# PEER's dense columns on one core: two output chunks per PSUM tile, a column-major first block, and a list and early products moved

## The chip, the cores and the metric

The kernel runs on one core of a Trainium2 chip. The metric is the device time of one execution in microseconds. The kernel before has three timed runs, with a median of 3780.73 us (3780.49 to 3784.08). All durations below come from one further execution that the hardware profiler recorded.

## What is computed

One residual block over 512 tokens of width 2048, then a final RMSNorm. The first half mixes tokens with two kinds of attention; the change doesn't touch it. The second half is PEER, which picks 16 of 16384 single-neuron experts for each token and head:

```python
def peer_ffn(h, w_query, sub_keys, expert_u, expert_v):
    ...
    scores = jnp.einsum('thpc,hpnc->thpn', q, sub_keys.astype(jnp.float32))
    s1, i1 = lax.top_k(scores[:, :, 0], PEER_TOPK)
    s2, i2 = lax.top_k(scores[:, :, 1], PEER_TOPK)
    ...
    top_score, pos = lax.top_k(cand_score, PEER_TOPK)
    expert_ids = jnp.take_along_axis(cand_id, pos, axis=-1)
    gates = jax.nn.softmax(top_score, axis=-1)
    ...
        u_sel = expert_u[idb]
        act = jax.nn.gelu(jnp.einsum('thkd,td->thk', u_sel, xb).astype(jnp.float32))
        w = (gb * act).astype(xb.dtype)
        v_sel = expert_v[idb]
        return jnp.einsum('thk,thkd->td', w, v_sel)
```

The output is `rms_norm(x + peer_ffn(rms_norm(x)))`.

## The kernel before

Activations are kept transposed: 16 chunks of 128 features on the partitions, tokens along the free axis. Every matrix product is done in three matmuls on split numbers (mm3, lines 116 to 118): hi weight by hi activation, hi by lo, lo by hi. A weight block of 128x2048 comes in two halves of 128x1024 (wload, from line 97). For each half a DMA issued by SyncE fills wr, ScalarE rounds it to wh (line 108), and VectorE subtracts to get wl (line 109). There are three buffers each for wh and wl, so a new half waits until PE has finished with an old one.

PEER is done in two ways. For the last 160 tokens the chosen expert rows are gathered by indirect DMAs, and VectorE multiplies each row of 128x2048 (lines 565 to 594). The function pace releases one such row at a time behind wl's and behind adds, so the rows fill VectorE while PE works. For the first 352 tokens (TD) everything is dense. The 16384 experts are 128 columns of 128:

- An up-product of column c is `expert_up(c)`: 48 matmuls of 352 columns into psu, then Gelu into a buffer gl. The first NS = 54 of the 128 are done early, inside the stages that choose the experts and scatter the gates, and their gl are spilled to DRAM (gact_sp). They are read back later by `fetch`. The rest run inside the down stage.
- `weigh(n)` multiplies gl by the gates of column n, which come from a DRAM matrix gsp (through gg, which lies in spare columns of h2), and splits the product into wg hi (ScalarE, line 825) and wg lo (VectorE, line 826). There are four gl buffers, so a spilled column is loaded only when an older one has been weighted.
- The down stage has 16 groups of GC = 8 columns. A group has eight weight blocks (jb), each with two output chunks (jj); the half w[jj] of a block holds chunk jj for all eight columns. A chunk sums 24 matmuls in psy, and VectorE adds it to acc (line 846). psy has four buffers of one PSUM bank.

A scheduler fixes the order of the instructions on each engine beforehand, from the order of the code, the buffers and its own costs. Each engine then takes its instructions strictly in that order.

The stages of PEER, in the profile's time: queries, and choose for the last 160 tokens, until 1578 us; the second loop over the heads, with choose for the 352 tokens and five early ups per head, until 1914; the transposes and the scatter, with one early up in two of three token blocks, until 2114; then the down stage until 3754, the final norm and the store.

Ahead of the second loop stand two pieces that the change moves. The first makes h2 from acc (lines 738 to 743, name h2n). The second builds the gather list of the 32 extra tokens (lines 748 to 763): rep and spread on VectorE, one product psrep on PE, and then idx_b, ggate_b and rstd_b out of it on VectorE.

The inner loop of the down stage, before:

```python
            for jj in range(JJ):
                j = jb * JJ + jj
                ps = (py, py2)[j % 2].tile([P, T], F32, tag="py", name="psy")
                for c in range(GC):
                    ...
                add = nc.vector.tensor_tensor(acc[:, j, :TD], acc[:, j, :TD], ps[:, :TD], op=ALU.add)
                pace(add, 1.0 / JJ)
```

Of the kernel before, what the change touches and what calls it, by code (L numbers as in the profile page):

```python
# [8 lines left out]
F32 = mybir.dt.float32  # L9
# [3 lines left out]
AF = mybir.ActivationFunctionType  # L13
ALU = mybir.AluOpType
# [4 lines left out]
P = 128  # L19
T = 512  # L20
NT = T // P
D = 2048
KC = D // P
# [17 lines left out]
HT = NT - 2  # L41
CW = 112
UPS = 5
NS = NH * UPS + TD // TB - -(-(TD // TB) // 3)
SLOW = 0.8
LEAD = 1
NP = 4
# [3 lines left out]
def block_kernel(ctx, tc, xT, gains, w_vf, bf, w_qk, w_v, w_g, w_br, w_o, w_q, keysT, uT, vP, expert_u, expert_v, outT):  # L51
# [63 lines left out]
    def mm3(ps, wh, wl, ah, al, start, stop):  # L115
        nc.tensor.matmul(ps, wh, ah, start=start, stop=False)  # L116
        nc.tensor.matmul(ps, wh, al, start=False, stop=False)  # L117
        nc.tensor.matmul(ps, wl, ah, start=False, stop=stop)  # L118
# [499 lines left out]
    def early(n, pace=None):  # L618
        for _ in range(n):
            if len(started) < NS:  # L620
                c = len(started)
                nc.scalar.dma_start(gact_sp[c], expert_up(c, pace))
                started.append(c)

    with ExitStack() as s1:
# [88 lines left out]
        for h in range(NH):  # L714
            sc = []
            sv = se.tile([P, 2, HT, NK], F32, tag="sv", name="sv")
            for p in range(2):
                b = 2 * h + p
                if b == 1:
                    norm2()  # L720
                if b == 3:
                    token_rows(lambda k: acc[:, k, T - P:], h2g, accg)
                ps = pu.tile([P, T], F32, tag="pu", name="psq2")
                proj(ps, wload(w_q[b]), h2)
                q = se.tile([P, T], F32, tag="ab1", name="q2")
                nc.scalar.activation(q, ps, AF.Copy)
                kt = se.tile([P, NK], F32, tag="kt", name="kt")
                nc.sync.dma_start(kt, keysT[b])
                ps = psx.tile([P, NT, NK], F32, tag="psx", name="pss")
                for t in range(NT):  # L730
                    nc.tensor.matmul(ps[:, t], q[:, t * P:(t + 1) * P], kt, start=True, stop=True)
                nc.scalar.activation(sv[:, p], ps[:, :HT], AF.Copy)
                sc.append(ps[:, HT:])
            nc.scalar.dma_start(scores[h], sv)
            choose(h, sc, HT, NT - HT)


        for k in range(KC):
            tmp = gl.tile([P, TD], F32, tag="gl", name="h2n")
            nc.vector.scalar_tensor_tensor(tmp, acc[:, k, :TD], g_sb[:, KC + k:KC + k + 1], rstd[:, :TD], op0=ALU.mult,  # L740
                                           op1=ALU.mult)
            nc.scalar.activation(h2[:, k, 0, :TD], tmp, AF.Copy)
            nc.vector.tensor_tensor(h2[:, k, 1, :TD], tmp, h2[:, k, 0, :TD].bitcast(F32), op=ALU.subtract)


        nc.vector.scalar_tensor_tensor(idx, ia[:, NT - 1], float(NK), ib[:, NT - 1], op0=ALU.mult, op1=ALU.add)
        nc.vector.tensor_copy(ggate, gt[:, NT - 1])
        rep = se.tile([P, 2 * HK + 2], F32, tag="ab1", name="rep")
        nc.vector.scalar_tensor_tensor(rep[:, :HK], ia[:, NT - 2], float(NK), ib[:, NT - 2], op0=ALU.mult, op1=ALU.add)
        nc.vector.tensor_copy(rep[:, HK:2 * HK], gt[:, NT - 2])  # L750
        nc.vector.tensor_copy(rep[:, 2 * HK:], rstd_t[:, NT - 2:NT - 1].to_broadcast([P, 2]))
        spread = se.tile([P, GB, MB], F32, tag="kt", name="spread")
        nc.vector.tensor_copy(spread, ident[:, P - MB:].unsqueeze(1).to_broadcast([P, GB, MB]))
        ps = psx.tile([P, T], F32, tag="psx", name="psrep")
        nc.tensor.matmul(ps[:, :2 * HK + 2], spread.rearrange("p g m -> p (g m)"), rep, start=True, stop=True)
        for g in range(GB):
            rows = slice(g * MB, (g + 1) * MB)
            nc.vector.tensor_copy(idx_b[rows], ps[rows, g * SB:(g + 1) * SB])
            nc.vector.tensor_copy(ggate_b[rows], ps[rows, HK + g * SB:HK + (g + 1) * SB])
        nc.vector.tensor_copy(rstd_b, ps[:, 2 * HK:2 * HK + 1])  # L760
        nc.vector.tensor_copy(sel_b, ident[:, :MB])
        for g in range(1, GB):
            nc.vector.tensor_tensor(sel_b, sel_b, ident[:, g * MB:(g + 1) * MB], op=ALU.add)


        for h in range(NH):
            sv = se.tile([P, 2, HT, NK], F32, tag="sv", name="svl")
            nc.sync.dma_start(sv, scores[h])
            choose(h, [sv[:, p] for p in range(2)], 0, HT)
            early(UPS, pace)  # L770

        tr = []
        for n, src in enumerate((ia, ib, gt)):
# [8 lines left out]
        for tb in range(TD // TB):  # L782
            st = se.tile([P, NK, TB], F32, tag="st", name="st")
            for t4 in range(0, TB, 4):
                tk = slice(tb * TB + t4, tb * TB + t4 + 4)
                ab = [se.tile([P, 4, NK], F32, tag=f"ab{i}", bufs=2, name="ab") for i in range(2)]
                nc.vector.tensor_tensor(ab[1], i128.unsqueeze(1).to_broadcast([P, 4, NK]),
                                        tr[1][:, tk].unsqueeze(2).to_broadcast([P, 4, NK]), op=ALU.is_equal)
                ps = pg.tile([P, 4, NK], F32, tag="pg", name="psgt")
                for i in range(4):  # L790
                    t = tb * TB + t4 + i
                    nc.vector.tensor_scalar(ab[0][:, i], i128, tr[0][:, t:t + 1], tr[2][:, t:t + 1], op0=ALU.is_equal,  # L792
                                            op1=ALU.mult)
                    nc.tensor.matmul(ps[:, i], ab[0][:, i], ab[1][:, i], start=True, stop=True)
                nc.scalar.activation(st[:, :, t4:t4 + 4].rearrange("p n t -> p t n"), ps, AF.Copy)
            nc.gpsimd.dma_start(gsp[:, tb], st)
            if tb % 3:
                early(1, pace)

    ex = pool("exp", 1)  # L800
    extra.append(ex)
# [31 lines left out]
    for grp in range(NG):  # L833
        while len(ws) < GC:
            ws.append(weigh(grp * GC + len(ws)))
        for jb in range(KC // JJ):
            w = wload(vP[grp, jb])
            for jj in range(JJ):
                j = jb * JJ + jj
                ps = (py, py2)[j % 2].tile([P, T], F32, tag="py", name="psy")  # L840
                for c in range(GC):
                    b = jj * GC + c
                    wh, wl = w[b // 8]
                    cc = slice(b % 8 * P, (b % 8 + 1) * P)
                    mm3(ps[:, :TD], wh[:, cc], wl[:, cc], ws[c][:, 0], ws[c][:, 1], c == 0, c == GC - 1)
                add = nc.vector.tensor_tensor(acc[:, j, :TD], acc[:, j, :TD], ps[:, :TD], op=ALU.add)
                pace(add, 1.0 / JJ)
        ws = []
    while todo:
        pace(add, 1.0)  # L850
# [81 lines left out]
```

## Time and profile before

| what | value |
|---|---|
| median of three runs | 3780.73 us |
| profiled execution: its own time | 3777.61 us |
| profiled execution: span | 3775.9 us |
| TensorE's mean granted clock | 0.988 of full |
| TensorE busy | 3670.2 us, 97%, 20745 matmuls |
| VectorE busy | 2597.2 us, 69% |
| ScalarE busy | 1290.8 us, 34% |
| DMA, mean over the span | 219 GB/s |

The busy share is taken over the span, which is what the profiler sees between the first and the last instruction. The execution's own time is 1.7 us longer. Matmuls overlap in the array, so the length printed for one is about twice its distance to the next.

### The profile page before, as it was taken

The numbers are of one execution on the slowest core, as the hardware profiler recorded it, in microseconds if no ns is written. First come the engines' busy times: TensorE is split into PE (matmuls) and PEld (weight loads), VectorE is DVE, ScalarE is ACT, GpSimd is POOL, SyncE is SP. The second block draws the span as 40 slices with busy tenths as digits, with TensorE's granted clock in tenths as the row PEclk, the third lists the DMA queues.
The fourth block names the chain that finished last, engine by engine and source line by source line (L and its number), as shares of the span: only waits on it lengthen the run. The fifth ranks groups of instructions, "written<-read, shape, count | busy, mean of one in ns | idle before, by whom it ended". The sixth has DMA issues, their size and how long they took to land.

```text
span 3775.9 us, 52068 instructions
## 1 busy us (share of the span) xinstructions
PE 3670.2 (97%) x20745; PEld 3381.2 (90%) x20745; DVE 2597.2 (69%) x3971; ACT 1290.8 (34%) x1824; POOL 530.6 (14%) x432
## 2 busy tenths in 40 slices
PE   9999999999999999899999898999999999999997
PEld 7888888888887878699999898999999999999997
DVE  5333445444555446899589888888789888988785
ACT  4334222232223223355356432333333333333333
POOL 0000000000000000011001122222223322322320
PEclk9999999999999999999999999999999999999999
DMA  4222222222224232377767899999889889989883
GB/s 142 79 78 77 98 95 95 87 90 81 88 95 138 95 101 97 106 267 275 274 245 274 290 340 326 353 342 331 318 334 372 327 334 337 366 330 343 327 306 110
DMA packets 233700, 827.25 MB, mean 219 GB/s; under 512 B 21736, under 2 KB 82664, under 8 KB 189680
## 3 DMA queue, kind: packets, MB, share of 16 engines
q1 hardware_dynamic: 174032, 450.30, 34.4%
q0 software_dynamic: 49920, 360.74, 24.9%
q10 hardware_dynamic: 9504, 12.88, 0.9%
q8 instruction: 163, 2.67, 0.3%
q14 instruction: 81, 0.66, 0.1%
HBM read 784.72 MB, written 39.11 MB: 218 GB/s over the span
## 4 chain that ended last, share of the span: by engine, by line
PE 83%; DVE 9%; DMA 4%; issue 2%; ACT 1%; SPq 0%; POOL 0%; DVEq 0%; POOLq 0%; ACTq 0%
PE psy L118 7%; PE psy L117 7%; PE psu L118 7%; PE psu L116 7%; PE psu L117 7%; PE psy L116 7%; PE psg L118 3%; PE psg L117 3%; PE psg L116 3%; PE psq L117 3%; PE psq L118 3%; PE psq L116 3%; DVE wl L109 2%; DVE ab L792 2%; PE psk L118 2%
## 5 line engine op out<-in xcount | busy, mean ns | idle before, releaser
L108 ACT ACTIVATE wh<-wr 128x1024 fp32r<-128x1024 f32 x768 | 813.8, 1060 | 1948.6 <-PE psy L117 583.1
L109 DVE TENSOR_TENSOR wl<-wr,wh 128x1024 fp32r<-128x1024 f32 x768 | 936.3, 1221 | 588.7 <-ACT wh L108 586.7
L116 PE MATMUL psy<-wg,wh 128*128 128x352 f32 x2048 | 667.5, 326 | 29.5 <-ACT wg L825 28.7
L117 PE MATMUL psy<-wg,wh 128*128 128x352 f32 x2048 | 670.5, 328 | 8.6 <-DVE wg L826 8.6
L118 PE MATMUL psu<-h,wl 128*128 128x352 f32 x2048 | 665.3, 325 | 12.8 <-DVE wl L109 12.7
L118 PE MATMUL psy<-wg,wl 128*128 128x352 f32 x2048 | 668.8, 328 | 7.4 <-DVE wl L109 7.2
L116 PE MATMUL psu<-h,wh 128*128 128x352 f32 x2048 | 666.5, 325 | 0.0
L117 PE MATMUL psu<-h,wh 128*128 128x352 f32 x2048 | 662.3, 323 | 0.0
L116 PEld LDWEIGHTS psy<-wg,wh 128*128 128x128 f32 x2048 | 389.8, 190 | 31.8 <-ACT wg L825 30.3
L117 PEld LDWEIGHTS psy<-wg,wh 128*128 128x128 f32 x2048 | 390.4, 191 | 10.5 <-DVE wg L826 10.4
L118 PEld LDWEIGHTS psu<-h,wl 128*128 128x128 f32 x2048 | 385.0, 188 | 16.3 <-DVE wl L109 16.3
L118 PEld LDWEIGHTS psy<-wg,wl 128*128 128x128 f32 x2048 | 389.7, 190 | 10.2 <-DVE wl L109 10.0
L117 PEld LDWEIGHTS psu<-h,wh 128*128 128x128 f32 x2048 | 386.2, 189 | 0.0
L116 PEld LDWEIGHTS psu<-h,wh 128*128 128x128 f32 x2048 | 385.9, 188 | 0.0
L558 POOL DMA_INDIRECT row<-eu,idx x128 | 180.8, 1413 | 903.0 <-DVE row L565 585.3
L583 DVE SCALAR_TENSOR_TENSOR acc<-row,gact,acc 128x2048 f32<-128x2048 f32 x128 | 300.2, 2346 | 9.3 <-DMA row<-ev,idx 9.2
L565 DVE SCALAR_TENSOR_TENSOR row<-row,rstd_t,h2g 128x2048 f32<-128x2048 f32 x128 | 300.3, 2346 | 0.0
L558 POOL DMA_INDIRECT row<-ev,idx x128 | 201.6, 1575 | 493.2 <-DVE acc L583 443.6
L116 PE MATMUL psq<-h,wh 128*128 128x512 f32 x512 | 205.2, 401 | 8.4 <-ACT wh L108 8.4
L117 PE MATMUL psq<-h,wh 128*128 128x512 f32 x512 | 206.1, 402 | 0.3 <-DVE h L167 0.3
L118 PE MATMUL psq<-h,wl 128*128 128x512 f32 x512 | 205.3, 401 | 0.1
L118 PE MATMUL psg<-h,wl 128*128 128x512 f32 x512 | 203.8, 398 | 0.0
(313 smaller groups left out, 5481.1 us busy)
## 6 DMA issues: line engine op xcount, KB each, us to landing
wr<-uT SPq DMA_DIRECT2D x256, 512.0 KB, 6.1
wr<-vP SPq DMA_DIRECT2D x256, 512.0 KB, 7.3
wr<-w_qk SPq DMA_DIRECT2D x64, 512.0 KB, 3.5
wr<-w_g SPq DMA_DIRECT2D x64, 512.0 KB, 3.5
gsp<-st POOLq DMA_DIRECT2D x22, 1024.0 KB, 4.5
wr<-w_br SPq DMA_DIRECT2D x32, 512.0 KB, 3.1
wr<-w_o SPq DMA_DIRECT2D x32, 512.0 KB, 3.2
wr<-w_q SPq DMA_DIRECT2D x32, 512.0 KB, 3.7
```

The lines of the kernel that those rows point to most:

```text
L108: nc.scalar.activation(hi, raw, AF.Copy)
L109: ins = nc.vector.tensor_tensor(lo, raw, hi.bitcast(F32), op=ALU.subtract)
L116: nc.tensor.matmul(ps, wh, ah, start=start, stop=False)
L117: nc.tensor.matmul(ps, wh, al, start=False, stop=False)
L118: nc.tensor.matmul(ps, wl, ah, start=False, stop=stop)
L558: nc.gpsimd.indirect_dma_start(out=row.rearrange("p k q -> p (k q)"), out_offset=None, in_=table, in_offset=bass.IndirectOffsetOnAxis(ap=i ...
L565: nc.vector.scalar_tensor_tensor(row, row, rstd_t[:, NT - 1:NT], h2g, op0=ALU.mult, op1=ALU.mult, accum_out=gact[:, i:i + 1])
L583: nc.vector.scalar_tensor_tensor(accg, row, gact[:, i:i + 1], accg, op0=ALU.mult, op1=ALU.add)
L792: nc.vector.tensor_scalar(ab[0][:, i], i128, tr[0][:, t:t + 1], tr[2][:, t:t + 1], op0=ALU.is_equal, op1=ALU.mult)
```

## The change

Five edits, none of which adds or removes a matmul:

1. MORE = 3: 57 up-products are early, not 54; the three more come after the scatter loop, and the first weighting after them.
2. h2n is written inside the first loop over the heads, ahead of the last head's choose.
3. The list of the 32 tokens becomes a function, second_list, which is called in the second loop after the first head's choose and its five early ups.
4. A weight block of the down stage has one psy tile of two neighbouring PSUM banks, one for each chunk. One VectorE instruction of 128x2x352 adds both, and pace is called once per block with 1.0 in place of twice with 0.5. There are two such tiles.
5. In the first block (jb = 0) of each group the matmuls go column by column: for each c, first chunk 0, then chunk 1. The other blocks keep chunk 0 in full before chunk 1.

```diff
+MORE = 3
+NS = NH * UPS + TD // TB - -(-(TD // TB) // 3) + MORE
...
+            if h == NH - 1:
+
+                for k in range(KC):
+                    tmp = gl.tile([P, TD], F32, tag="gl", name="h2n")
...
             choose(h, sc, HT, NT - HT)
...
+        def second_list():
...
             choose(h, [sv[:, p] for p in range(2)], 0, HT)
             early(UPS, pace)
+            if h == 0:
+                second_list()
...
             if tb % 3:
                 early(1, pace)
 
+        early(MORE, pace)
+
...
             w = wload(vP[grp, jb])
-            for jj in range(JJ):
-                j = jb * JJ + jj
-                ps = (py, py2)[j % 2].tile([P, T], F32, tag="py", name="psy")
-                for c in range(GC):
-                    b = jj * GC + c
-                    wh, wl = w[b // 8]
-                    cc = slice(b % 8 * P, (b % 8 + 1) * P)
-                    mm3(ps[:, :TD], wh[:, cc], wl[:, cc], ws[c][:, 0], ws[c][:, 1], c == 0, c == GC - 1)
-                add = nc.vector.tensor_tensor(acc[:, j, :TD], acc[:, j, :TD], ps[:, :TD], op=ALU.add)
-                pace(add, 1.0 / JJ)
+            ps = py2.tile([P, JJ, T], F32, tag="py", name="psy")
+            order = [(jj, c) for c in range(GC) for jj in range(JJ)]
+            for jj, c in (order if jb == 0 else sorted(order)):
+                b = jj * GC + c
+                wh, wl = w[b // 8]
+                cc = slice(b % 8 * P, (b % 8 + 1) * P)
+                mm3(ps[:, jj, :TD], wh[:, cc], wl[:, cc], ws[c][:, 0], ws[c][:, 1], c == 0, c == GC - 1)
+            out = acc[:, jb * JJ:(jb + 1) * JJ, :TD]
+            add = nc.vector.tensor_tensor(out, out, ps[:, :, :TD], op=ALU.add)
+            pace(add, 1.0)
```

The change also moves instructions on the engines. Three places follow; the number behind a name tells its buffer, and is another in each program.

The first place is PE's order at the start of the early ups, before. psu_11806 is the first up-product, wl_11816 the lo part of its second weight half:

```order
L116 MATMUL psu_11806<-h2_8494,wh_11815 128x352
L117 MATMUL psu_11806<-h2_8494,wh_11815 128x352
L116 MATMUL psu_11870<-h2_8494,wh_11873 128x352
L117 MATMUL psu_11870<-h2_8494,wh_11873 128x352
L755 MATMUL psrep_11701<-rep_11695,spread_11699 128x258
L118 MATMUL psu_11806<-h2_8494,wl_11816 128x352
L116 MATMUL psu_11806<-h2_8494,wh_11815 128x352
```

The same place in the changed kernel, where psu_11785 is the first up-product and wl_11795 the lo part of its second half:

```order
L117 MATMUL psu_11785<-h2_8494,wh_11794 128x352
L118 MATMUL psu_11785<-h2_8494,wh_11794 128x352
L117 MATMUL psu_11849<-h2_8494,wh_11852 128x352
L118 MATMUL psu_11849<-h2_8494,wh_11852 128x352
L119 MATMUL psu_11785<-h2_8494,wl_11795 128x352
L117 MATMUL psu_11785<-h2_8494,wh_11794 128x352
L118 MATMUL psu_11785<-h2_8494,wh_11794 128x352
```

Only psrep has gone from between the matmuls; it now stands some 210 rows later, between two up-products. The lo matmul behind it is in its old place.

The second place is VectorE's order at the entry of the down stage, before. gl_17235 is the first column to be weighted:

```order
L792 TENSOR_SCALAR ab_17214<-i128_9669,ia_9664,gt_9666 128x128 x4
L109 TENSOR_TENSOR wl_17361<-wr_17358,wh_17360 128x1024
L822 TENSOR_TENSOR gl_17235<-gl_17235,h2_8494 128x352
L822 TENSOR_TENSOR gl_17237<-gl_17237,h2_8494 128x352
L822 TENSOR_TENSOR gl_17249<-gl_17249,h2_8494 128x352
L826 TENSOR_TENSOR wg_17243<-gl_17235,wg_17243 128x352
```

In the changed kernel, wl_17372 belongs to the last early up, wl_17492 and wl_17498 to the first down block, wl_17560 to the second, and gl_17433 is the first column to be weighted:

```order
L110 TENSOR_TENSOR wl_17372<-wr_17369,wh_17371 128x1024
L110 TENSOR_TENSOR wl_17492<-wr_17489,wh_17491 128x1024
L110 TENSOR_TENSOR wl_17498<-wr_17495,wh_17497 128x1024
L110 TENSOR_TENSOR wl_17560<-wr_17557,wh_17559 128x1024
L830 TENSOR_TENSOR gl_17433<-gl_17433,h2_8494 128x352
L830 TENSOR_TENSOR gl_17435<-gl_17435,h2_8494 128x352
L834 TENSOR_TENSOR wg_17441<-gl_17433,wg_17441 128x352
L830 TENSOR_TENSOR gl_17447<-gl_17447,h2_8494 128x352
```

Both halves of the first down block, and the first half of the second one, now stand ahead of the first weighting.

The third place is VectorE's order at the start of the fourth group, before. wg_19064 is its fourth column, wl_19094 the lo part of the second half of its first block; the add of psy_19005 is of the group before:

```order
L846 TENSOR_TENSOR acc_79<-acc_79,psy_19005 128x352
L565 SCALAR_TENSOR_TENSOR row_19031,gact_9641<-row_19031,rstd_t_78,h2g_9639 128x2048
L826 TENSOR_TENSOR wg_19064<-gl_19055,wg_19064 128x352
L822 TENSOR_TENSOR gl_19061<-gl_19061,h2_8494 128x352
L822 TENSOR_TENSOR gl_19067<-gl_19067,h2_8494 128x352
L822 TENSOR_TENSOR gl_19073<-gl_19073,h2_8494 128x352
L826 TENSOR_TENSOR wg_19070<-gl_19061,wg_19070 128x352
L826 TENSOR_TENSOR wg_19076<-gl_19067,wg_19076 128x352
L826 TENSOR_TENSOR wg_19082<-gl_19073,wg_19082 128x352
L109 TENSOR_TENSOR wl_19094<-wr_19091,wh_19093 128x1024
L846 TENSOR_TENSOR acc_79<-acc_79,psy_19097 128x352
```

The same start in the changed kernel; wl_19238 and wl_19244 are the two halves of the group's first block:

```order
L834 TENSOR_TENSOR wg_19214<-gl_19205,wg_19214 128x352
L110 TENSOR_TENSOR wl_19238<-wr_19235,wh_19237 128x1024
L854 TENSOR_TENSOR acc_79<-acc_79,psy_19131 128x2x352
L566 SCALAR_TENSOR_TENSOR row_19181,gact_9641<-row_19181,rstd_t_78,h2g_9639 128x2048
L830 TENSOR_TENSOR gl_19211<-gl_19211,h2_8494 128x352
L830 TENSOR_TENSOR gl_19217<-gl_19217,h2_8494 128x352
L830 TENSOR_TENSOR gl_19223<-gl_19223,h2_8494 128x352
L834 TENSOR_TENSOR wg_19220<-gl_19211,wg_19220 128x352
L834 TENSOR_TENSOR wg_19226<-gl_19217,wg_19226 128x352
L834 TENSOR_TENSOR wg_19232<-gl_19223,wg_19232 128x352
L110 TENSOR_TENSOR wl_19244<-wr_19241,wh_19243 128x1024
```

The second half's wl is behind the three gl and the three wg in both, but the column order now needs that half from the first column on. The four wg of the columns before stand ahead of the gather row, and no longer one of them behind it. The fifth group starts in the same order; the second, third, sixth and seventh have both halves' wl ahead of the wg.

## Rows read from the trace of the kernel before

**Rows 1.** The page, part 1: busy time, share of the span and instructions.

```profile
PE 3670.2 (97%) x20745; PEld 3381.2 (90%) x20745; DVE 2597.2 (69%) x3971; ACT 1290.8 (34%) x1824; POOL 530.6 (14%) x432
```

**Rows 2.** Stretches of the down stage: length, each engine's busy time, clock, DMA share, GB/s.

```profile
2129.00:2133.00 4.00, 4.00 (x14) 3.73 (x14) 3.33 (x8) 1.61 (x5) 0.00 (x0) 0.52 0.50 146
2133.00:2400.00 267.00, 249.92 (x1501) 247.94 (x1500) 229.97 (x274) 78.20 (x91) 69.65 (x45) 0.97 0.92 332
2400.00:2620.00 220.00, 211.13 (x1273) 208.65 (x1272) 189.77 (x225) 67.25 (x80) 59.16 (x39) 0.98 0.94 345
2620.00:3692.00 1072.00, 1065.70 (x6601) 1061.92 (x6600) 884.26 (x789) 351.06 (x423) 300.49 (x191) 1.00 0.89 333
```

**Rows 3.** PE's waits: total us, times, longest.

```profile
PE psy L116 <- ACT wg L825: 28.7, 6, 14.3
...
PE psrep L755 <- DVE rep L749: 11.2, 1, 11.2
PE psy L117 <- DVE wg L826: 8.6, 4, 5.1
```

**Rows 4.** PE's timeline from 1584 us: start, length, instruction, [idle before <-releaser].

```profile
1595.53 1.20 PE L755 MATMUL psrep<-rep,spread 128*128 128x258 f32 x2 [11.21 <-DVE rep L749]
1601.98 0.66 PE L118 MATMUL psu<-h,wl 128*128 128x352 f32 x1 [5.25 <-DVE wl L109]
```

**Rows 5.** VectorE's timeline in the same stretch.

```profile
1597.12 0.16 DVE L758 CAST idx_b<-psrep 32x32 uint32<-32x32 f32 x1
...
1598.40 0.08 DVE L646 MATCH_VALUE_LOAD i<-v,tk 128x8 f32 x1
...
1600.72 1.21 DVE L109 TENSOR_TENSOR wl<-wr,wh 128x1024 fp32r<-128x1024 f32 x1
```

**Rows 6.** PE's timeline at 1687 us.

```profile
1687.33 0.43 PE L118 MATMUL psu<-h,wl 128*128 128x352 f32 x1 [1.61 <-DVE wl L109]
```

**Rows 7.** Timeline of all engines at the entry of the down stage.

```profile
2114.42 1.03 ACT L795 ACTIVATE st<-psgt 128x512 f32<-128x512 f32 x1 [0.58 <-PE psgt L794]
...
2123.05 0.37 SPq L820 DMA_DIRECT2D h<-gsp  x1
2127.60 1.40 DVE L822 TENSOR_TENSOR gl<-gl,h 128x352 f32<-128x352 f32 x3 [12.63 <-DMA h<-gsp]
...
2128.71 0.66 PE L116 MATMUL psy<-wg,wh 128*128 128x352 f32 x1 [14.33 <-ACT wg L825]
```

**Rows 8.** Timelines at the start of the third group; last row: of the fourth.

```profile
2260.80 2.62 SPq L807 DMA_DIRECT2D gl<-gact_sp  x4
...
2268.63 1.40 DVE L822 TENSOR_TENSOR gl<-gl,h 128x352 f32<-128x352 f32 x3 [3.77 <-DMA gl<-gact_sp]
2269.95 1.39 DVE L826 TENSOR_TENSOR wg<-gl,wg 128x352 fp32r<-128x352 f32 x3
...
2269.74 0.66 PE L116 MATMUL psy<-wg,wh 128*128 128x352 f32 x1 [3.66 <-ACT wg L825]
...
2342.21 0.66 PE L117 MATMUL psy<-wg,wh 128*128 128x352 f32 x1 [5.07 <-DVE wg L826]
```

**Rows 9.** The page's costliest groups: busy us, mean ns | idle before.

```profile
L108 ACT ACTIVATE wh<-wr 128x1024 fp32r<-128x1024 f32 x768 | 813.8, 1060 | 1948.6 <-PE psy L117 583.1
L109 DVE TENSOR_TENSOR wl<-wr,wh 128x1024 fp32r<-128x1024 f32 x768 | 936.3, 1221 | 588.7 <-ACT wh L108 586.7
...
L565 DVE SCALAR_TENSOR_TENSOR row<-row,rstd_t,h2g 128x2048 f32<-128x2048 f32 x128 | 300.3, 2346 | 0.0
```

**Rows 10.** VectorE's groups by line, from 2128 us to the end.

```profile
L846 DVE TENSOR_TENSOR acc<-acc,psy 128x352 f32<-128x352 f32 x256 | 132.4, 517 | 79.0 <-PE psy L118 79.0
...
L861 DVE TENSOR_TENSOR fin<-fin 128x512 f32<-128x512 f32 x15 | 10.3, 686 | 2.3 <-ACT fin L860 2.3
```

**Rows 11.** The page's DMA issues: count, KB each, median us to landing.

```profile
gact_sp<-gl ACTq DMA_DIRECT2D x54, 176.0 KB, 3.9
gl<-gact_sp SPq DMA_DIRECT2D x54, 176.0 KB, 6.2
```

More of the change, by code (lines that the diff above doesn't have):

```diff
@@ L43 @@
 UPS = 5
-NS = NH * UPS + TD // TB - -(-(TD // TB) // 3)
+MORE = 3
+NS = NH * UPS + TD // TB - -(-(TD // TB) // 3) + MORE
 SLOW = 0.8
@@ L734, in block_kernel @@
             nc.scalar.dma_start(scores[h], sv)
-            choose(h, sc, HT, NT - HT)
[L738 to L743, printed above, removed]
+            if h == NH - 1:
+                for k in range(KC):
+                    tmp = gl.tile([P, TD], F32, tag="gl", name="h2n")
+                    nc.vector.scalar_tensor_tensor(tmp, acc[:, k, :TD], g_sb[:, KC + k:KC + k + 1], rstd[:, :TD], op0=ALU.mult,
+                                                   op1=ALU.mult)
+                    nc.scalar.activation(h2[:, k, 0, :TD], tmp, AF.Copy)
+                    nc.vector.tensor_tensor(h2[:, k, 1, :TD], tmp, h2[:, k, 0, :TD].bitcast(F32), op=ALU.subtract)
@@ L746, in block_kernel @@
+            choose(h, sc, HT, NT - HT)
         nc.vector.scalar_tensor_tensor(idx, ia[:, NT - 1], float(NK), ib[:, NT - 1], op0=ALU.mult, op1=ALU.add)
         nc.vector.tensor_copy(ggate, gt[:, NT - 1])
[L748 to L763, printed above, removed]
+        def second_list():
+            rep = se.tile([P, 2 * HK + 2], F32, tag="ab1", name="rep")
+            nc.vector.scalar_tensor_tensor(rep[:, :HK], ia[:, NT - 2], float(NK), ib[:, NT - 2], op0=ALU.mult, op1=ALU.add)
+            nc.vector.tensor_copy(rep[:, HK:2 * HK], gt[:, NT - 2])
+            nc.vector.tensor_copy(rep[:, 2 * HK:], rstd_t[:, NT - 2:NT - 1].to_broadcast([P, 2]))
+            spread = se.tile([P, GB, MB], F32, tag="kt", name="spread")
+            nc.vector.tensor_copy(spread, ident[:, P - MB:].unsqueeze(1).to_broadcast([P, GB, MB]))
+            ps = psx.tile([P, T], F32, tag="psx", name="psrep")
+            nc.tensor.matmul(ps[:, :2 * HK + 2], spread.rearrange("p g m -> p (g m)"), rep, start=True, stop=True)
+            for g in range(GB):
+                rows = slice(g * MB, (g + 1) * MB)
+                nc.vector.tensor_copy(idx_b[rows], ps[rows, g * SB:(g + 1) * SB])
+                nc.vector.tensor_copy(ggate_b[rows], ps[rows, HK + g * SB:HK + (g + 1) * SB])
+            nc.vector.tensor_copy(rstd_b, ps[:, 2 * HK:2 * HK + 1])
+            nc.vector.tensor_copy(sel_b, ident[:, :MB])
+            for g in range(1, GB):
+                nc.vector.tensor_tensor(sel_b, sel_b, ident[:, g * MB:(g + 1) * MB], op=ALU.add)
```

## The prediction

> **What bounds the kernel now.** I read the page first, for what is full: TensorE is busy 97% of the span [rows 1], and no edit takes a matmul away. So the change can only win back idle PE time (106 us in all) or time at the half clock, and I look for where that lies. The view of stretches gives the places [rows 2]: in the long middle of the down stage PE works 1065.7 of 1072 us at full clock, while its first 487 us (2133 to 2620) lose 17.1 + 8.9 us of idle time, and the clock of 0.97 and 0.98 costs another 0.03 x 267 + 0.02 x 220 = 12.4 us. From the same view I take PE's pace: 1072 us hold 6601 matmuls, 0.162 us each, so a block of 48 takes 7.8 us and a chunk of 24 takes 3.9 us. Then the view of PE's waits, for who ends the idle time [rows 3]: the hi part of the weighted activations (28.7 us in six waits, one of 14.3), their lo part (8.6 us in four), and the matrix of the second list (11.2 us, once). The timelines of these three places show what stood behind each, and that decides what the change can do to it.
>
> **The list moved (second_list, h2n).** PE stops for 11.2 us before psrep, which waits for rep; then it stops 5.25 us more for a wl [rows 4]. Taking psrep away does not let PE go: the next matmul needs that wl, and the order of the changed kernel has the same row there, behind the same steps of choose. VectorE runs without a gap until it reaches that wl at 1600.72 [rows 5]; only the thirteen instructions of the list go from in front of it. Nine of them take 1598.40 - 1597.12 = 1.28 us [rows 5], the other four I put at 0.5 us from rows of like size: 1.8 us. So I take 1.8 us off, not 11.2. Behind it stand waits of the same kind, such as 1.61 us at 1687 [rows 6]; VectorE has less ahead of them, and I take 1.7 us as half of two such waits. The list comes back after the first five up-products, in running work: PE does one psrep there without a wait by the order, but VectorE pays the 1.8 us. h2n keeps its place in the issued order, so I cost its move at nothing: the choose of the last head covers it as before; without that cover it would be late by a few of its steps. **A: -3.5 us** (ends: 0, if the list only shifts the waits, and -11.2, the named wait).
>
> **Three more early up-products.** Before, PE's last scatter matmul is followed by a chain: the last st on ScalarE at 2114.42, its store, the read of the gates issued at 2123.05, gl at 2127.60, PE at 2128.71 [rows 7]. That is 14.3 us idle, and then 4 us at clock 0.52 [rows 2], 1.9 us more: 16.2 us. Now 3 x 48 matmuls, 23 us, stand behind the last scatter matmul, longer than the chain, so the read of the gates is hidden. What is late next is the first weighting. The order puts the wl of block 1 ahead of gl and wg on VectorE, and its wh waits for the last up-product: 1.06 for wh + 1.22 for wl [rows 9] + 1.1 from gl to PE [rows 7] = 3.4 us. The gl buffer of the fourth column is that of the last spill: store 3.9 and load 6.2 us [rows 11], 10.1 us after the last Gelu, when PE has had 3.4 us of wait and three columns of six matmuls (2.9 us): about 3.8 us more. With a microsecond at the half clock: 8.2 us. The three spills, their loads and 3 x 1 MB of uT only change place. **B: -8 us** (ends: -13 if only the first wait stays, +1 if the fourth and the eighth column both wait in full and the clock falls as before).
>
> **First block of a group, column by column.** At a group start the gl loads of the last three columns are issued when earlier columns free their buffers, at 2260.80 for the third group; gl runs at 2268.63 and PE, which stopped, goes on at 2269.74 [rows 8]. The six starts cost 14.4 + 8.6 us idle [rows 3] and 12.4 of clock, 35 us, 5.9 each. The load's time does not change, only how far PE gets before it needs it: by the order 23 to 25 matmuls before, 32 now, 1.3 us. That is -5.2 us at four starts. At the fourth and fifth group the order now has the second weight half's wl behind the three gl and three wg, and column-major work needs it after 7 matmuls. The wg end at 2269.95 + 1.39 = 2271.34 [rows 8], wl 1.22 later, 2272.56; that is 2.8 us after PE's restart, and PE has stopped 17 matmuls (2.7 us) earlier: 5.5 us more than such a start. The fifth pays it, +5.5. The fourth had a second wait of 5.07 us before, at 2342 [rows 8], so it lost some 12.4 us (5.9 + 5.1 and more clock), and 5.9 + 5.5 is -1 there. The column order also frees the first weight slot only at the block's end, so the wl of block 1's second half comes behind the add and the gather rows: 0.89 (the wide add, below) + 2.35 per row + 1.22 [rows 9], against 26 matmuls, 4.2 us, until PE needs it (a chunk of 24, and two of the next that take only wh). With one row that is 0.3 us, at 12 starts 3.6; with two rows, as in the first, fourth and seventh group, 2.6 us, together 7.8. **C: -5.2 + 5.5 - 1 + 3.6 + 7.8 = +10.7 us** (ends: -10, where the clock stays full at four starts and no row is in the way, and +28, if eight more starts lose 2.2 us).
>
> **One add over two banks.** Between the add of 128x352 (517 ns) [rows 10] and wl of 128x1024 (1221 ns) [rows 9] a row of 704 columns lies at 887 ns, so 128 adds save 128 x (2 x 517 - 887) = 19 us of VectorE, which is no bound here. PE's waits hold none on an add, before; I cost the new tile at nothing, because PE meets the same tile again a whole block (7.8 us) later and the add takes 0.9 of it. Before, three chunks (11.7 us) lay between, so the cover shrinks to 6.9 us. Here the Trainium skill speaks against the change: Perfetto Trace Analysis, Optimizing Tensor Performance, wants independent matmul groups to rotate through different PSUM banks, so that evacuating one overlaps the next. By that rule four turns are better than two pairs, and an add held up for more than the 6.9 us would stop PE; no run here shows it yet, and it is a rival below. At the end the last add covers both chunks: 0.37 us longer, and the squares' sum of one more chunk (0.69 us [rows 10]) comes behind it. **D: +1 us.**
>
> **Sum.** -3.5 - 8 + 10.7 + 1 = +0.2 us on the profiled execution of 3777.6 us (span 3775.9 and 1.7 around it). That execution lies 3.1 us under the median of the runs, 3780.7; so 3780.9 us for a median.
>
> **The rivals.** A measurement of this kernel tells about 0.2%, 7.6 us, from no change.
> - *The starts heal.* The four ordinary starts keep their full clock, 5.9 to 2.4 us each (-14), no row is in the way of a wl, the entry keeps only its first wait (-12): -3.5 - 12 - 14 + 4.5 + 1 = -24, 3757 us. For it: the 1.61 us wait [rows 6] shows that idle times can be short; against: the load itself is no faster. Chance 0.31.
> - *All named waits go*, as the parts are written: 28.7 + 8.6 + 11.2 [rows 3] and 14.3 of clock, 3719 us. Against it stand the wl behind psrep and the loads. 0.05.
> - *Gather rows in front of the wl* (slower). A row on VectorE lasts 2.35 us and waits for its gather; it stands between the wide add and the wl at nearly every start. It decides where the two take over 4.2 us. If eight of the one-row starts lose as two-row starts do: 8 x 2.2 = +18, 3799 us. For it: the margin is only 0.3 us. 0.18.
> - *The two tiles* (slower). An add behind three gl that wait for their load, 3.77 us as at the third group [rows 8], six times, beyond the 6.9 us of cover: +23, 3804 us. The rule of the Trainium skill's Perfetto Trace Analysis, above, points this way. 0.05.
> - That the list does not do what it is meant to is in the forecast.
>
> **How the numbers follow.** The forecast, no change that can be told, has 0.41: 3773 to 3788. Faster holds 0.31 + 0.05 = 0.36, slower 0.18 + 0.05 = 0.23. The range 3752 to 3800 takes in the healed starts and the rows in the way, and leaves out the ceiling, most of the banks' case and the ends of C.
>
> **What would show it.** Right: the gap after 1584 still ends on a wl, at about 16 us; at the entry PE waits some 8 us instead of 14.3, in pieces, with more than one releaser; the fourth and fifth group stop for 9 us on a wl; after the first block short waits on wl appear in the first, fourth and seventh group; psrep waits for nothing. Wrong: a gap at 1584 of 5 us or less; no wait at the entry; group starts at full clock; or psy waiting for an add.

## The result: 1.4% slower, outside the range

The changed kernel takes 3832.83 us (median of four runs, 3827.67 to 3839.15), the kernel before 3782.10 beside it: 51 us slower by the medians, whose quotient is 1.0134. The measured ratio, estimated from all runs, is 1.0139 (interval 1.0126 to 1.0152), which is 53 us. The forecast was no change, 3780.9 us, with a range of 3752 to 3800. The profiled execution of the changed kernel has a span of 3826.0 us against 3775.9, so the two traces hold 50.1 us of the difference.

The stretches of the changed kernel's down stage (columns as in [rows 2]: length, busy time of PE, PEld, VectorE, ScalarE, POOL, clock, DMA share, GB/s):

```profile
2150.00:2400.00 250.00, 226.54 (x1324) 222.75 (x1325) 205.32 (x220) 69.51 (x81) 81.88 (x40) 0.95 0.87 319
2400.00:2620.00 220.00, 196.64 (x1140) 193.15 (x1140) 173.46 (x185) 60.88 (x72) 71.00 (x35) 0.93 0.85 314
2620.00:3692.00 1072.00, 1049.77 (x6442) 1044.44 (x6441) 871.34 (x717) 337.71 (x404) 332.29 (x195) 0.99 0.89 334
```

In the same 1072 us PE now does 6442 matmuls, not 6601 [rows 2], and the two stretches ahead have a lower clock too. Its waits (total us, times, longest), against [rows 3]:

```profile
PE psy L119 <- DVE wl L110: 41.2, 17, 7.7
PE psu L119 <- DVE wl L110: 32.0, 16, 15.6
PE psy L117 <- ACT wg L833: 20.7, 5, 5.6
...
PE psy L118 <- DVE wg L834: 2.7, 3, 2.1
```

The waits for wg became shorter, 37.3 us before and 23.4 now, and psrep waits for nothing. What has come in their place are waits for wl, the lo part of the weights: 73.2 us in two of these lines. Before, the same two had 19.9:

```profile
PE psu L118 <- DVE wl L109: 12.7, 10, 5.2
...
PE psy L118 <- DVE wl L109: 7.2, 6, 2.1
```

To place the 50.1 us, I take the time from the first down matmul of each of the 16 groups to that of the next, less 0.1615 us (the distance of two matmuls when nothing is waited for) for each matmul in it. This is idle time and half clock together. It sums to 48.6 us before and to 108.6 us now: +60.0. The entry gives back 11.3: the first down matmul is at 2140.7 in place of 2128.7, but 144 more matmuls (23.3 us) lie ahead of it. The end is 1.4 us longer. -11.3 + 60.0 + 1.4 = +50.1. The loss by groups:

| group | 1 | 2 | 3 | 4 | 5 | 6 | 7 | 8 | 9 to 16, sum |
|---|---|---|---|---|---|---|---|---|---|
| before, us | 2.3 | 6.9 | 5.5 | 12.5 | 4.3 | 6.3 | 3.3 | 0.9 | 6.8 |
| changed, us | 6.6 | 6.8 | 6.7 | 18.7 | 15.8 | 7.3 | 12.3 | 6.5 | 27.9 |

**The list.** The wait for rep is gone, and PE stops nearly as long as with the two waits before (11.21 and 5.25 us), now for the wl (PE's timeline, against [rows 4]):

```profile
1600.99 0.66 PE L119 MATMUL psu<-h,wl 128*128 128x352 f32 x1 [15.62 <-DVE wl L110]
```

**The entry.** PE waits 5.62 us for the first weighted column, not 14.33 [rows 7]; then the clock is at its lower level again, 0.50 from 2140.7 to 2143.7 us. In the same list stands the first group's wait behind two gather rows:

```profile
2140.68 0.66 PE L117 MATMUL psy<-wg,wh 128*128 128x352 f32 x1 [5.62 <-ACT wg L833]
2157.78 0.66 PE L119 MATMUL psy<-wg,wl 128*128 128x352 f32 x1 [2.12 <-DVE wl L110]
```

**The start of the fourth group.** VectorE's timeline, and then PE's: the wl of the second half ends only after the three gl and three wg, and PE, which is in the first column, waits 7.67 us for it. At the fifth group it is 7.72 us.

```profile
2350.54 0.52 DVE L830 TENSOR_TENSOR gl<-gl,h 128x352 f32<-128x352 f32 x1
2351.21 0.53 DVE L830 TENSOR_TENSOR gl<-gl,h 128x352 f32<-128x352 f32 x1 [0.15 <-DMA gl<-gact_sp]
2353.70 0.53 DVE L830 TENSOR_TENSOR gl<-gl,h 128x352 f32<-128x352 f32 x1 [1.97 <-DMA gl<-gact_sp]
2354.15 1.39 DVE L834 TENSOR_TENSOR wg<-gl,wg 128x352 fp32r<-128x352 f32 x3
2355.45 2.35 DVE L110 TENSOR_TENSOR wl<-wr,wh 128x1024 fp32r<-128x1024 f32 x2
...
2356.72 0.66 PE L119 MATMUL psy<-wg,wl 128*128 128x352 f32 x1 [7.67 <-DVE wl L110]
```

**The second block of most later groups.** The eighth group begins at 2713.5, so PE's first block ends at 2721.3. VectorE then stands in a gl that waits for a gate read: it is the first column of the *next* group, weighed ahead. Only after it and its wg come the wide add, a gather row, and the wl. ScalarE, in order too, has that wg ahead of the three wh. The timelines of the three engines in one, by time:

```profile
2722.77 0.53 DVE L830 TENSOR_TENSOR gl<-gl,h 128x352 f32<-128x352 f32 x1 [6.88 <-DMA h<-gsp]
...
2723.33 0.50 ACT L833 ACTIVATE wg<-gl 128x352 fp32r<-128x352 f32 x1 [8.35 <-DVE gl L830]
2723.73 2.94 ACT L109 ACTIVATE wh<-wr 128x1024 fp32r<-128x1024 f32 x3
...
2723.86 0.53 DVE L834 TENSOR_TENSOR wg<-gl,wg 128x352 fp32r<-128x352 f32 x1 [0.57 <-ACT wg L833]
2724.30 0.88 DVE L854 TENSOR_TENSOR acc<-acc,psy 128x704 f32<-128x704 f32 x1
2725.10 2.35 DVE L575 SCALAR_TENSOR_TENSOR row<-row,rstd_b,h2g 128x2048 f32<-128x2048 f32 x1
...
2727.37 3.49 DVE L110 TENSOR_TENSOR wl<-wr,wh 128x1024 fp32r<-128x1024 f32 x3
...
2728.65 0.43 PE L119 MATMUL psy<-wg,wl 128*128 128x352 f32 x1 [2.29 <-DVE wl L110]
```

The same rows stand around 2982, 3237 and 3494 (groups 10, 12 and 14), with waits of 2.2 to 2.3 us; groups 13 and 15 wait 2.0 and 2.1 us. In these six groups the gl starts 0.8 to 1.7 us after the first block's end. In groups 9 and 11 it starts about 1 us before that end, the same add, row and wl follow, and PE doesn't wait. The ninth group's first block ends at 2851.8 (VectorE's timeline):

```profile
2850.80 0.53 DVE L830 TENSOR_TENSOR gl<-gl,h 128x352 f32<-128x352 f32 x1 [4.36 <-DMA h<-gsp]
...
2852.34 0.88 DVE L854 TENSOR_TENSOR acc<-acc,psy 128x704 f32<-128x704 f32 x1
2853.13 2.35 DVE L584 SCALAR_TENSOR_TENSOR acc<-row,gact,acc 128x2048 f32<-128x2048 f32 x1
2855.40 1.22 DVE L110 TENSOR_TENSOR wl<-wr,wh 128x1024 fp32r<-128x1024 f32 x1
```

The late gl needs the row for its effect. Without the row's 2.27 us the eighth group's wl would have ended at about 2726.3, just when PE stopped (an estimate from the rows above).

**The up-products of the later groups.** From 2120 us on they wait 10.8 us for a wl, in six waits; the kernel before has one of 1.1 us. Before one of them three gather rows stand between the wide add and the wl, and the third has to wait for its gather (PE's waits, the first line of the kernel before; then VectorE's timeline and PE's):

```profile
PE psu L118 <- DVE wl L109: 1.1, 1, 1.1
PE psu L119 <- DVE wl L110: 10.8, 6, 2.4
...
2778.86 0.89 DVE L854 TENSOR_TENSOR acc<-acc,psy 128x704 f32<-128x704 f32 x1 [1.74 <-PE psy L119]
2779.67 2.34 DVE L575 SCALAR_TENSOR_TENSOR row<-row,rstd_b,h2g 128x2048 f32<-128x2048 f32 x1
...
2781.94 2.35 DVE L575 SCALAR_TENSOR_TENSOR row<-row,rstd_b,h2g 128x2048 f32<-128x2048 f32 x1
...
2785.24 2.35 DVE L575 SCALAR_TENSOR_TENSOR row<-row,rstd_b,h2g 128x2048 f32<-128x2048 f32 x1 [0.94 <-DMA row<-eu,idx_b]
...
2787.51 1.22 DVE L110 TENSOR_TENSOR wl<-wr,wh 128x1024 fp32r<-128x1024 f32 x1
...
2788.79 0.43 PE L119 MATMUL psu<-h,wl 128*128 128x352 f32 x1 [1.95 <-DVE wl L110]
```

### The profile page after: what moved, and what is told of

Its sections match the earlier page's. It is cut to its first block, busy times and chain, and to the rows that moved or that the text cites. A ratio compares the mean times of both kernels' runs of the same rounds, so it can differ in the third digit from the quotient of the medians.

```text
span 3826.0 us, 52053 instructions
## 1 busy us (share of the span) xinstructions
PE 3690.2 (96%) x20745; PEld 3396.4 (89%) x20745; DVE 2588.7 (68%) x3843; ACT 1284.9 (34%) x1822; POOL 590.6 (15%) x432
## 4 chain that ended last, share of the span: by engine, by line
PE 75%; DVE 11%; DMA 6%; issue 5%; ACT 1%; POOL 1%; SPq 1%; DVEq 0%; POOLq 0%; ACTq 0%
PE psy L119 6%; PE psy L118 6%; PE psy L117 6%; PE psu L119 6%; PE psu L117 6%; PE psu L118 5%; PE psg L118 3%; PE psg L119 3%; PE psg L117 3%; PE psq L118 3%; PE psq L119 3%; PE psq L117 3%; DVE wl L110 2%; DMA gl<-gact_sp 2%; DVE ab L798 2%
## 5 line engine op out<-in xcount | busy, mean ns | idle before, releaser
L117 PE MATMUL psy<-wg,wh 128*128 128x352 f32 x2048 | 673.8, 329 | 21.9 <-ACT wg L833 20.7
L117 PEld LDWEIGHTS psy<-wg,wh 128*128 128x128 f32 x2048 | 394.4, 193 | 25.8 <-ACT wg L833 22.4
L118 PEld LDWEIGHTS psy<-wg,wh 128*128 128x128 f32 x2048 | 394.5, 193 | 4.9 <-DVE wg L834 4.7
L559 POOL DMA_INDIRECT row<-eu,idx x128 | 217.7, 1701 | 900.4 <-DVE row L566 556.6
L559 POOL DMA_INDIRECT row<-ev,idx x128 | 219.9, 1718 | 491.8 <-DVE acc L584 466.5
```

The costliest lines, as they stand in the source:

```text
L559: nc.gpsimd.indirect_dma_start(out=row.rearrange("p k q -> p (k q)"), out_offset=None, in_=table, in_offset=bass.IndirectOffsetOnAxis(ap=i ...
```

## The experiments

Three theories were put up. The column order of the first block is the cost, because both weight halves are held until the block's end (theory 1). The wide add with its one release of gather rows per block is the cost (theory 2). The shift from 54 to 57 early products is the cost (theory 3). Ratios below are to the kernel before on the same chip, whose medians lay between 3778.0 and 3780.8 us in these runs. "Loss" is the sum over the 16 groups as above, from the profiled execution alone, which can lie up to 10 us from its run's median.

### Each edit undone, and each alone

The old chunk order in the changed kernel:

```diff
-            for jj, c in (order if jb == 0 else sorted(order)):
+            for jj, c in sorted(order):
```

> The changed kernel with one edit undone: the first block of a group again takes chunk 0 in full before chunk 1. Theory 1 (the column order holds both weight halves until the block's end, so the wl of the second block comes late in every group, and in the fourth and fifth group the first block itself waits for the second half): the 16 groups lose 108.6 us in the changed kernel and 48.6 before; most of the 60 us goes, and the entry's gain of some 11 us stays: 3770 to 3790 us. Theory 2 (one add and one release per block bunch the gather rows in front of the wl): little changes, 3815 to 3835 us. Theory 3 (57 early products instead of 54 shift the loads of the groups): little changes, 3815 to 3835 us.

3801.63 us, ratio 1.0058 (1.0041 to 1.0075), loss 82.8 us. The order costs 31 us in the changed kernel, but 23 us stay: more than one theory is at work.

The add narrow and the release split, with the two-bank tile and the column order kept:

```diff
-            out = acc[:, jb * JJ:(jb + 1) * JJ, :TD]
-            add = nc.vector.tensor_tensor(out, out, ps[:, :, :TD], op=ALU.add)
-            pace(add, 1.0)
+            for jj in range(JJ):
+                out = acc[:, jb * JJ + jj, :TD]
+                add = nc.vector.tensor_tensor(out, out, ps[:, jj, :TD], op=ALU.add)
+                pace(add, 1.0 / JJ)
```

> The changed kernel with one edit undone in part: the two-bank tile stays, but each chunk has its own add, and rows are released by 0.5 after each add. Theory 1: within 10 us of the changed kernel's 3833, since the weight halves are still freed at the block's end. Theory 2: the rows spread again, the waits of 2.3 us on a wl in front of up-products (2786, 2922, 3175, 3432) go and those of the first blocks shrink: 3785 to 3805 us.

3823.62 us, ratio 1.0121 (1.0104 to 1.0138), loss 104.8. Only 9 us come back (7 by the ratios). PE now also waits for an add, which neither the kernel before nor the changed one shows (PE's waits):

```profile
PE psy L117 <- DVE acc L855: 9.4, 6, 2.5
```

The two-bank tile is free only after its second add, and here a gather row stands between the two. So this run is no clean test of theory 2. The up-products' waits for a wl do fall with the release split, from 10.8 to 4.0 us.

The column order alone on the kernel before, with single-bank tiles:

```diff
-                for c in range(GC):
-                    b = jj * GC + c
...
+            order = [(jj, c) for c in range(GC) for jj in range(JJ)]
+            for jj, c in (order if jb == 0 else sorted(order)):
```

> The kernel before with the column order in the first block alone, on two single-bank tiles, each with its own add. Theory 1: slower by 35 to 60 us, 3815 to 3840 us. Theory 2 and theory 3: within 10 us of before, 3772 to 3792 us.

3803.43 us, ratio 1.0061 (1.0044 to 1.0078), loss 75.2: 25 us alone, less than theory 1 said. Most of the extra loss is in the later groups: on the second block's wl, groups 8 to 15 wait 21.9 us together, against 5.0 in the kernel before. The stops of 7.7 us at the fourth and fifth group are not in this run. In [rows 2]'s last stretch PE does 205 matmuls fewer:

```profile
2620.00:3692.00 1072.00, 1046.11 (x6396) 1040.72 (x6395) 873.60 (x772) 338.58 (x407) 292.65 (x191) 0.99 0.89 329
```

The two-bank tile, one add and one release alone, in the old order:

```diff
-                add = nc.vector.tensor_tensor(acc[:, j, :TD], acc[:, j, :TD], ps[:, :TD], op=ALU.add)
-                pace(add, 1.0 / JJ)
+            out = acc[:, jb * JJ:(jb + 1) * JJ, :TD]
+            add = nc.vector.tensor_tensor(out, out, ps[:, :, :TD], op=ALU.add)
+            pace(add, 1.0)
```

> The kernel before with the two-bank tile, one add and one release per block alone, in the old chunk order. Theory 1: within 10 us of before, 3772 to 3792 us. Theory 2: slower by 30 to 50 us, 3810 to 3830 us, with waits of some 2.3 us on a wl that stands behind two or three gather rows.

3796.51 us, ratio 1.0048 (1.0031 to 1.0065), loss 64.6: 18 us. Theory 1 alone is refuted, and theory 2 gets a part, though a smaller one than it claimed.

### The early products, the list, the release

```diff
+MORE = 3
-NS = NH * UPS + TD // TB - -(-(TD // TB) // 3)
+NS = NH * UPS + TD // TB - -(-(TD // TB) // 3) + MORE
...
+        early(MORE, pace)
```

> The kernel before with 57 early up-products instead of 54, alone. If the entry of the down stage gains what the changed kernel showed (the first down product comes 11 us earlier, counted in work) and nothing is given back: 3765 to 3770 us. If the wait only moves into the first groups, whose later columns then wait for their gl and wg (the first group lost 10.0 us in the changed kernel with the old chunk order, 2.3 before): 3774 to 3783 us.

3771.79 us, ratio 0.9980 (0.9970 to 0.9989): 6 us faster, loss 55.7. Some of the entry's gain goes back into the groups, as the second case said, but not all. Theory 3 is refuted: these products help.

The list and h2n moved, as in the changed kernel, nothing else:

> The kernel before with h2n and the list of the 32 tokens moved, alone. If the named wait for rep was the cost: 11 us faster, 3766 to 3769 us. If the wl behind it is what PE needs: the gap after 1584 still lasts some 16 us and the time is 3774 to 3779 us.

3779.21 us, ratio 0.9999 (0.9990 to 1.0008). No difference, and PE's timeline is that of the changed kernel:

```profile
1601.08 0.66 PE L119 MATMUL psu<-h,wl 128*128 128x352 f32 x1 [15.61 <-DVE wl L110]
```

The wait on rep (11.21 us) and the wait on wl (5.25 us) of [rows 4] became one wait of 15.6 us.

The release alone, with narrow adds on single banks:

```diff
-                pace(add, 1.0 / JJ)
+            pace(add, 1.0)
```

> The kernel before with the gather rows released once per block, after the second chunk's add, with 1.0 in place of twice 0.5; tiles, adds and chunk order as before. The two-bank tile with one add cost 18 us alone. If the bunched release is what costs in it: 3790 to 3800 us. If the wide add or the two tiles cost by themselves: 3775 to 3783 us.

3793.51 us, ratio 1.0039 (1.0025 to 1.0054), loss 66.1: 15 us, against the wide add's 18. The two intervals overlap, so a cost of the wide tile beside the release isn't shown. The marks are the same in both runs: from 2120 us on the up-products wait 12.9 us for a wl here and 13.6 with the wide add (1.1 before, 0.2 with the column order alone), and the sixth group loses 18.4 and 16.9 us (6.3 before). Rows in a row also meet gathers that haven't landed. With the wide add alone, VectorE stands still for 4.87 us in front of one, and PE then waits 5.31 us for the wl queued behind (VectorE's timeline and PE's):

```profile
2544.81 2.35 DVE L565 SCALAR_TENSOR_TENSOR row<-row,rstd_t,h2g 128x2048 f32<-128x2048 f32 x1 [4.87 <-DMA row<-eu,idx]
...
2548.39 0.88 DVE L846 TENSOR_TENSOR acc<-acc,psy 128x704 f32<-128x704 f32 x1
2549.19 2.35 DVE L565 SCALAR_TENSOR_TENSOR row<-row,rstd_t,h2g 128x2048 f32<-128x2048 f32 x1
...
2551.90 1.22 DVE L109 TENSOR_TENSOR wl<-wr,wh 128x1024 fp32r<-128x1024 f32 x1
...
2553.17 0.66 PE L118 MATMUL psu<-h,wl 128*128 128x352 f32 x1 [5.31 <-DVE wl L109]
```

### The halves by column

If the order costs because both halves are held, it should cost nothing when the first half of the first block's weights holds columns 0 to 3 for both chunks and the second half columns 4 to 7. This takes another layout of the weights in DRAM and another index:

```diff
-                b = jj * GC + c
+                b = c * JJ + jj if jb == 0 else jj * GC + c
...
+    first = out["vP"][:, 0].reshape(NG, P, JJ, GC, P).transpose(0, 1, 3, 2, 4).reshape(NG, P, D)
+    out["vP"] = np.concatenate([first[:, None], out["vP"][:, 1:]], axis=1)
```

> The column order in the first block, alone on the kernel before as in the run that cost 25 us, but the two halves of that block's weights hold columns 0 to 3 and 4 to 7, each for both chunks, so that the first half is freed after 24 matmuls and the second is needed only then. If the column order costs because both halves are held to the block's end: the 25 us go, 3770 to 3782 us. If it costs by itself (two open sums, the add of both chunks at the end): 3795 to 3808 us.

3774.36 us, ratio 0.9983 (0.9974 to 0.9992), loss 47.7. The 25 us are gone, and the order even gains 4.

> The changed kernel with one mend: the first block's halves by column; wide add with one release per block, list and three more early products stay. If holding both halves to the block's end is the whole cost of the column order here too: 3790 to 3803 us, level with the run that undid the order (3802). If not: 3810 us or more.

3777.99 us, ratio 0.9998 (0.9988 to 1.0007), loss 61.0. That is better than expected: one mend takes all of the 51 to 54 us, wide add and bunched release left in place. What it doesn't take are the up-products' waits for a wl, 10.9 us in six. At the eighth group VectorE waits in the same gl, but the wl follows at once, ahead of wg, add and row, since its slot was freed 24 matmuls earlier (VectorE's timeline):

```profile
2695.06 0.53 DVE L830 TENSOR_TENSOR gl<-gl,h 128x352 f32<-128x352 f32 x1 [7.12 <-DMA h<-gsp]
2695.51 1.22 DVE L110 TENSOR_TENSOR wl<-wr,wh 128x1024 fp32r<-128x1024 f32 x1
2696.64 0.52 DVE L834 TENSOR_TENSOR wg<-gl,wg 128x352 fp32r<-128x352 f32 x1
2697.08 0.88 DVE L854 TENSOR_TENSOR acc<-acc,psy 128x704 f32<-128x704 f32 x1
2697.87 2.35 DVE L575 SCALAR_TENSOR_TENSOR row<-row,rstd_b,h2g 128x2048 f32<-128x2048 f32 x1
```

The changed kernel with narrow tiles, adds and releases, and the column order on the old halves:

> The changed kernel with the wide add undone in full: four single banks, an add and a release of 0.5 per chunk; column order, list and three more early products stay. If the parts add (column order 25, three more -6, list 0): 3793 to 3802 us. If the column order with the three more early products costs more than the two alone: 3805 to 3820 us.

3801.51 us, ratio 1.0058 (1.0037 to 1.0080), loss 89.3. Here the parts add: 25 - 6 + 0. So what the wide add costs depends on its company: 31 us on top of this one, 18 alone. Two kinds of wait are absent from this trace: those of the up-products for a wl (none from 2120 us on), and the stops of 7.7 us at the fourth and fifth group, which lose 9.8 us together here and 34.5 in the changed kernel. Whether the tile or the release brings those stops wasn't tested.

### Other places for the rows

With the wide add alone, the rows were released behind each wl of a block:

```diff
-            w = wload(vP[grp, jb])
+            w = wload(vP[grp, jb], pace=pace)
...
-            pace(add, 1.0)
```

> The kernel before with the two-bank tile and one add, in the old chunk order, but the rows of the down blocks are released by 0.5 after each of a block's two wl instead of 1.0 after its add. If the place of the rows, ahead of the wl that PE needs next, is what the wide add's 18 us were: 3770 to 3782 us. If the tile or the add costs by itself: 3790 to 3800 us.

3815.04 us, ratio 1.0104 (1.0088 to 1.0120): a miss, worse than the bunched release. Then, half in the middle of the block, behind the last matmul of chunk 0:

```diff
+                if jj < JJ - 1:
+                    pace(last, 1.0 / JJ)
...
-            pace(add, 1.0)
+            pace(add, 1.0 / JJ)
```

> The kernel before with the two-bank tile and one add, in the old chunk order, with rows released by 0.5 after the last matmul of the first chunk and by 0.5 after the add, so at the rate of the kernel before. If the bunched release alone was the wide add's 18 us: 3768 to 3784 us. If a wide add behind which every row and wl queues costs by itself as well: 3785 to 3800 us.

3855.22 us, ratio 1.0207 (1.0191 to 1.0223): far off both theories. The rows now stand ahead of their gathers all through the stage. VectorE's groups by line show 56.5 us of idle time in front of them, where the kernel before has none:

```profile
L565 DVE SCALAR_TENSOR_TENSOR row<-row,rstd_t,h2g 128x2048 f32<-128x2048 f32 x85 | 199.6, 2349 | 56.5 <-DMA row<-eu,idx 56.5
```

Both places were also tried in the changed kernel with its halves by column. Behind wl:

> The changed kernel in full, with the two mends: the first block's halves by column, and the rows released after each wl. If these two were what made it slower: 3760 to 3775 us, 58 to 73 us under the changed kernel. If half of the loss has another cause: about 3800 us.

3795.17 us, ratio 1.0062 (1.0042 to 1.0082). In the middle of the block:

> The changed kernel in full, with the first block's halves by column, and the rows released by 0.5 in the middle of a block and 0.5 after its add. If halves held too long and bunched rows are the whole loss: 3762 to 3775 us, level with or under the kernel before. If there is a third cause: 3785 us or more.

3833.06 us, ratio 1.0145 (1.0119 to 1.0171). Both are slower than the halves alone (3778). They don't show a third cause in the change, since each release costs by itself. Whether a wide add could keep the old kernel's places for its rows was not found.

### What beats both

Three more early products and the halves by column, on the kernel before:

> The two parts that gained alone, three more early up-products (-6 us) and the column order with halves by column (-4 us), on the kernel before. If the gains add: 3766 to 3770 us. If both reach for the same waits of the first groups: 3770 to 3775 us.

3765.95 us, ratio 0.9967 (0.9957 to 0.9977): 12 us faster than before and 67 under the changed kernel. The gains of the two parts add. The changed kernel with halves by column differs from this one by the wide add with its release, and by the list, whose move made no difference alone. So the wide add still costs about 12 us there (0.9998 against 0.9967), and its six waits of up-products, 10.9 us, are not in this kernel.

## Why the prediction was wrong, step by step

- **What bounds the kernel** held: all of the 50 us is PE waiting or at its lower clock, and no engine became full (VectorE's busy time fell by 8.5 us, to 2588.7).
- **A, the list: -3.5 forecast, no difference measured** (0.9990 to 1.0008 is -4 to +3 us, which just holds -3.5). The mechanism was right: psrep was no loss of its own, and the gap "still ends on a wl, at about 16 us". It was 15.6.
- **B, three more early products: -8 forecast, -6 measured alone** (interval -11 to -4). The chain was hidden, as worked out, and the first weighting was late next: 5.62 us in the changed kernel, in place of 3.4. The 3.8 us more for the fourth column didn't come: behind its first matmul, PE's longest wait in the first group is 0.88 us in the run with this edit alone. Instead the 16 groups together lost 7.1 us more, 4.6 of them in the seventh, whose columns are now all read back. So the sum is near in part by luck.
- **C, the column order: +10.7 forecast, +25 alone and +31 in the changed kernel.** This step failed, in three terms. The waits came where they were forecast: the fourth and fifth group stop on the wl of the second half (7.67 and 7.72 us; "for 9 us" was said), and the three starts with two rows wait 2.12, 4.71 and 2.28 us on the second block's wl, where 2.6 each was said.

  But the price of the fourth and fifth group was too low: 5.5, -1, 2.6 and 0.3 make +7.4 us, and their loss rose by 17.7, from 16.8 to 34.5, half clock after the stops included. The "-5.2 us at four starts" was not won: the starts with such waits were five, not six (groups 2 to 6), and groups 2, 3 and 6, which the stops leave alone, lose 20.8 us, against 18.7 before.

  The third mis-sized term is the one-row start, "0.3 us, at 12 starts 3.6". I let the add begin at the block's end. But VectorE was then in the gl of the next group's first column, which waited for a gate read and started only at 2722.77, 1.5 us later, and with its wg the add began only at 2724.30, 3 us after the block's end. So six of the later one-row starts wait 2.0 to 2.3 us each, nearly like two-row starts; where the gl came before the block's end, in groups 9 and 11, PE doesn't wait. My rival "gather rows in front of the wl" had that size (eight starts by 2.2 us) and the place, but it blamed the rows alone; the late gl ahead of the add used up the margin, and the row then made the wl late. The run with halves by column fits: the same gl waits, the same row follows the add, and PE doesn't wait, because the wl no longer stands behind them.
- **D, the wide add: +1 forecast, +18 alone.** Its price was right, 886 ns against 887:

```profile
L854 DVE TENSOR_TENSOR acc<-acc,psy 128x704 f32<-128x704 f32 x128 | 113.4, 886 | 122.6 <-PE psy L119 119.9
```

  "I cost the new tile at nothing" was right as to the tile: the changed kernel has no wait of PE on an add. The rule of the Trainium skill's Perfetto Trace Analysis (Optimizing Tensor Performance: rotate matmul groups through different PSUM banks) did bite where the tile stayed wide and the adds were split, 9.4 us in six waits (with the column order on four single banks there are two, 1.9 us); the rival on the banks was not what made the change slower. The step that failed is an omission: I counted the add's time and left out the release. pace was called once with 1.0 in place of twice with 0.5, so, counted in the traces, 31 of the 128 adds now have two or three gather rows (4.7 us and more) queued behind them, where one of 256 had before, and a wl mostly comes next. That alone is 15 us on the kernel before. Its mark, the waits of up-products on a wl, is 10.8 us in the changed kernel; the forecast had no term for it.
- **The sum.** The parts alone make 0 - 6 + 25 + 18 = +37 us; together they make 51 to 54: the wide add costs 31 us beside the column order, and 18 alone. The trace shows one thing that needs both: the stops of 7.7 us at the fourth and fifth group, whose loss is 34.5 us together in the changed kernel, 14.5 with the order alone and 15.1 with the wide add alone. That this is the whole of the difference isn't shown. The range stopped at one slower case, 3800, as if the costs of C and of the rows couldn't come together.

## What to carry to other kernels

Before reordering a matmul loop, ask which buffers the new order holds longer, and who refills them: a loop that uses two buffers in turn frees neither until its end. If the data's layout follows the loop (here, halves by column), the order need not cost anything; here it gained 4 us. On an in-order engine the price of a step is what may stand ahead of it, waits included; a margin of a few tenths of a microsecond behind a DMA is no margin. A call that releases other work is part of an edit, and has to be costed as the work it releases.

## What the runs showed of the hardware

PE's clock after a wait does not follow from the wait's length alone. After the 2.12 us wait at 2157.78 and after the 7.67 us wait at 2356.72 it was at its lower level, but after the 2.29 us wait at 2728.65 it stayed at full level (stretches of the changed kernel):

```profile
2158.00:2161.00 3.00, 3.00 (x11) 3.00 (x12) 3.00 (x5) 0.50 (x1) 1.68 (x1) 0.50 0.97 337
2357.00:2360.00 3.00, 3.00 (x11) 3.00 (x12) 0.80 (x1) 0.00 (x0) 0.00 (x0) 0.50 0.95 266
2728.80:2731.80 3.00, 3.00 (x19) 3.00 (x20) 2.07 (x2) 0.00 (x0) 0.61 (x1) 1.00 0.68 184
```

So a stall of the same size costs 2.3 us in one place and at least 1.3 more in another (11 matmuls in the 3 us behind it, where 19 were done at full level, at 0.16 us each). From the lengths of waits alone, a forecast of this kernel can only bound that cost from both sides.
